# Gate and up products of pairs of inner tiles by Strassen's scheme (seven half-width products for eight), and the inner layer in groups of eight tiles

## Chip, core and metric

The kernel runs on one core of a Trainium2 chip. The metric is device time in microseconds (us) of one execution. Engine names are those of the profile: PE is the matrix engine (PEld its weight load), DVE the vector engine, ACT the scalar engine, POOL the general-purpose engine, SP the engine whose queue issues most transfers.

## What is computed

Six layers (four of a first block, two of a second) of a residual network over 512 positions and 1024 features, in float32. Each layer adds a mixer (attention, a state-space layer, a pooling layer or a hybrid) and then a gated feed-forward part to `x`. Only the feed-forward part is touched by the change; it has 2816 inner features:

```python
def swiglu(h, w_gate_up, w_down):
    g, u = jnp.split(h @ w_gate_up, 2, axis=-1)
    return (jax.nn.silu(g) * u) @ w_down
...
        x = x + swiglu(rms_norm(x, ffn_norm_g[i]), ffn_w_gate_up[i], ffn_w_down[i]).astype(x.dtype)
```

## The kernel before

**Layout.** Everything is kept feature-major: a tile has 128 features in the partitions and the 512 positions in the free dimension. `x` is eight such tiles (`KD` = 8); the inner layer of the feed-forward part has 22 (`KF` = 22).

**Three products for one.** A float32 operand is split into a high part rounded to the matrix engine's reduced format and a low part, the rest. `p3` multiplies high by high, high by low and low by high into one accumulator, so each 128x128 weight tile costs three matmuls of 512 columns. The split of the weights is made on the chip: a chunk `wraw` of eight weight tiles (128x1024 floats, 512 KB) comes by a transfer on SP's queue, ACT copies it to the high part `wh` (`w_h`), and DVE subtracts to get the low part `wl` (`w_l`). Chunks are used in strict order; `w_upto` keeps up to four of them in flight.

**The feed-forward part** (`ffn`). For each inner tile f a gate product `pg` and an up product `pu` are accumulated over the eight feature tiles (24 matmuls each). `close` then multiplies the gate by the row of reciprocal norms `rstd` (DVE), applies silu (ACT), multiplies by the up product (DVE), multiplies by `rstd` again (POOL, line 367) and `keep` splits the result into `ph` and `pl`, which hold all 22 inner tiles. When all are there, the down product runs: eight output tiles `po`, each over 22 inner tiles (66 matmuls), each added to `x`, after which the next layer's normalised tiles `Xh`, `Xl` are made. In the two layers of the second block the norm is applied beforehand, and `close` has no `rstd`.

**Side work.** Independent work of other layers is cut into steps in a queue `bg`, and `bgstep(nbg)` runs some of them in `close` and after each output tile. During the first layer these are the state-space layer's tables (names beginning with `s5`); during the next two they are products for the second block's modulation: DVE instructions `adaj` that each read a 256 KB transfer `adaw`, with two buffers for it.

**Order.** The instructions of each engine are executed in the order in which the program lists them; an engine that waits for one instruction starts none behind it. A scheduler of the framework moves instructions of one engine past each other where no data forbids it. The third layer's feed-forward part has a `lead`: the pooling mixer's steps run between the products of its first three inner tiles.

Of the kernel before, what the change touches and what calls it, by code (L numbers as in the profile page):

```python
# [20 lines left out]
P = 128  # L21
# [10 lines left out]
NH = 1  # L32
HALF = CH // NH
SLOTS = 8
NCHUNK = 541
# [35 lines left out]
def kernel(  # L71
# [55 lines left out]
    st = {"slot": 0, "dma": 1, "h": 0, "l": 0}  # L127
    raws, hs, ls = {0: wraw0}, {}, {}

    def w_dma(c):  # L130
        raws[c] = wp.tile([P, CH], F32, name="wraw", tag="wraw", bufs=4)
        sp.dma_start(raws[c], wst[c])

    def half(c):
        return raws[c // NH][:, c % NH * HALF:(c % NH + 1) * HALF]

    def w_h(c):
        hs[c] = wp.tile([P, HALF], F32R, name="wh", tag="wh", bufs=3 * NH)
        a.activation(hs[c], half(c), AF.Copy)  # L139

    def w_l(c):
        ls[c] = wp.tile([P, HALF], F32R, name="wl", tag="wl", bufs=2 * NH)
        v.tensor_tensor(out=ls[c], in0=half(c), in1=hs[c].bitcast(F32), op=ALU.subtract)  # L143

    def w_upto(c):
        last = wst.shape[0] - 1
        for key, ahead, end, make in (("dma", c // NH + 3, last, w_dma), ("h", c + 3 * NH - 1, NH * last + NH - 1, w_h),
                                      ("l", c + 2 * NH - 1, NH * last + NH - 1, w_l)):
            while st[key] <= min(ahead, end):
                make(st[key])  # L150
                st[key] += 1

    def wnext(n, *ks):
        s0 = st["slot"]
        hn = SLOTS // NH
        assert len(ks) == n and s0 // hn == (s0 + n - 1) // hn
        c, o = divmod(s0, hn)
        if o == 0 or c not in hs:
            w_upto(c)
        keys.extend(ks)  # L160
        st["slot"] += n
        sl = slice(o * P, (o + n) * P)
        return hs[c][:, sl], ls[c][:, sl]
# [11 lines left out]
    def mm(o, l, r, s0, s1):  # L175
        pe.matmul(o, lhsT=l, rhs=r, start=s0, stop=s1)  # L176

    def p3(o, l, r, first, last):
        mm(o, l[0], r[0], first, False)
        mm(o, l[0], r[1], False, False)  # L180
        mm(o, l[1], r[0], False, last)
# [164 lines left out]
    def ffn(name_gu, name_dn, lay, deferred, post, nbg=3, lead=None, ada=None):  # L346
        with tc.tile_pool(name="ffn", bufs=1, reuse_waits="tile") as fp:
            ph = fp.tile([P, KF, S], F32R, name="ph")
            F0 = 3
            plo = [fp.tile([P, F0, S], F32R, name="pl0")]  # L350
            R = {}

            def pl(f):
                if f >= F0 and len(plo) == 1:
                    plo.append(fp.tile([P, KF - F0, S], F32R, name="pl1", tag="pl1", bufs=1))
                return plo[0][:, f, :] if f < F0 else plo[1][:, f - F0, :]

            def tmp():
                return fp.tile([P, S], F32, name="t1", tag="t1", bufs=3)

            def close(f, pg, pu):
                t_ = tmp()
                if deferred:
                    v.tensor_tensor(out=t_, in0=pg, in1=R["r"], op=ALU.mult)  # L364
                    a.activation(t_, t_, AF.Silu)
                    v.tensor_tensor(out=t_, in0=pu, in1=t_, op=ALU.mult)  # L366
                    g_.tensor_tensor(out=t_, in0=t_, in1=R["r"], op=ALU.mult)  # L367
                else:
                    a.activation(t_, pg, AF.Silu)
                    v.tensor_tensor(out=t_, in0=pu, in1=t_, op=ALU.mult)  # L370
                keep(f, t_)

            def keep(f, t_):
                a.activation(ph[:, f, :], t_, AF.Copy)
                v.tensor_tensor(out=pl(f), in0=t_, in1=ph[:, f, :].bitcast(F32), op=ALU.subtract)
                bgstep(nbg)
# [4 lines left out]
            def gu(t, which, f, k):  # L381
                p3(t, wnext(1, gu_key(which, f, k)), xk(k), k == 0, k == KD - 1)

# [15 lines left out]
            if lead:  # L399

                f0 = F0
                steps = lead(fp.tile([P, (KF - F0) * S], F32, name="lroom", tag="pl1", bufs=1), tmp)
# [10 lines left out]
            for f in range(f0, KF):  # L413
                pg, pu = acc("pg"), acc("pu")
                for which, t in enumerate((pg, pu)):
                    for k in range(KD):
                        gu(t, which, f, k)
                    if deferred and "c" not in R and not lead:
                        R["c"] = rstd_cols(nrm["sq"])
                    elif deferred and "r" not in R:  # L420
                        R["r"] = keep_rstd(rstd_rows(R["c"]))
                close(f, pg, pu)
            for m in range(KD):
                po = acc("po")
                for f in range(KF):
                    w = wnext(1, ("t", name_dn, lay, f * P, m * P))
                    p3(po, w, (ph[:, f, :], pl(f)), f == 0, f == KF - 1)
                post(m, po)
                bgstep(nbg)
# [640 lines left out]
    def pool_lead(lay, fin):  # L1070
# [5 lines left out]
        def lead(room, tmp):  # L1076
            bufs_ = [room[:, i * W_:(i + 1) * W_] for i in range(17)]
            for t_ in bufs_:
                g_.memset(t_[:, :PAD], 0.0)
            rest = room[:, 17 * W_:]  # L1080
# [651 lines left out]
    for m in range(KD):  # L1732
        split_scaled(m, col("mix_g", m), False)
        if m == 1:
            w_h(0)
            w_l(0)
            st["h"] = st["l"] = 1
# [23 lines left out]
    if stage():  # L1761
        ffn("ffn_w_gate_up", "ffn_w_down", 1, True, then(add_x, fd("mix_g", 2)))
    if stage() and stage():
        ffn("ffn_w_gate_up", "ffn_w_down", 2, True, then(add_x, fd("mix_g", 3)), lead=pool_lead(0, fd("ffn_g", 2)))
# [8 lines left out]
    if stage():  # L1773
        ffn("ffn_w_gate_up", "ffn_w_down", 3, True, then(add_x, mixer[0].post if upto > 8 else None))
    for lay in range(2):
        if stage():
            hybrid(lay, then(gated(lay, 2), feed[lay].post), mixer[lay])
        if stage():
            ffn("w_gate_up_2", "w_down_2", lay, False, then(gated(lay, 5), mixer[1].post if lay == 0 else None), ada=feed[lay])
# [143 lines left out]
```

## Time and profile before

| | us |
|---|---|
| median of 3 runs | 3521.31 (3516.45 to 3531.56) |
| the profiled execution's own time | 3519.53 |
| its span, first to last instruction | 3517.8 |
| granted clock of PE, mean over the span | 0.992 of full speed |
| PE busy in the span | 3450.8 |
| DVE busy in the span | 1978.5 |

The busy time of an engine is the time in which at least one of its instructions was under way. A matmul's record lasts longer than the step from one matmul to the next, since they are pipelined: what one costs is read from starts, not from durations. The same holds, less strongly, for DVE.

### The profile page before, as it was taken

Reading aid. Unit: us, or ns where it says so; the run is one execution under the profiler, and the core shown is the slowest. Engines: PE = TensorE matmul, PEld = TensorE weight load, DVE = VectorE, ACT = ScalarE, POOL = GpSimd, SP = SyncE. Lnnn points to the kernel's source line nnn. Section 1 sums busy time; section 2 is a strip of 40 time slices with the busy share of each in tenths; the row PEclk is TensorE's granted clock in tenths of the full one; section 3 lists DMA queues with packets and bytes.
Section 4 is the critical chain, followed back from the end, with each engine's and each line's share of the span. In section 5 each row is a group of like instructions: output and inputs, shape, how many; then the busy total and the mean of one; then the engine's idle time right before and its main releaser. Section 6 shows DMA issues by size and latency. Waiting matters only on the chain.

```text
span 3517.8 us, 44670 instructions
## 1 busy us (share of the span) xinstructions
PE 3450.8 (98%) x16676; PEld 2848.3 (81%) x16676; DVE 1978.5 (56%) x3826; ACT 1333.0 (38%) x2127; POOL 503.6 (14%) x595
## 2 busy tenths in 40 slices
PE   8999999989999989999999999999999999999999
PEld 6887778888888868888788888877888887788887
DVE  8876786365555577554766433386643337664332
ACT  4553333323332233223554333356432225643221
POOL 1102443021111031100001221122100002210000
PEclk9999999999999999999999999999999999999999
DMA  4422344483455425544322222221132222113232
GB/s 153 112 70 91 117 134 140 142 271 115 137 172 170 149 98 179 168 156 146 127 73 69 96 96 96 90 93 37 49 102 96 96 90 94 37 49 102 96 104 82
DMA packets 189145, 395.26 MB, mean 112 GB/s; under 512 B 57552, under 2 KB 84320, under 8 KB 186880
## 3 DMA queue, kind: packets, MB, share of 16 engines
q1 hardware_dynamic: 186592, 375.61, 33.1%
q10 hardware_dynamic: 2304, 16.78, 1.4%
q8 instruction: 131, 2.15, 0.3%
q14 instruction: 86, 0.70, 0.1%
q0 software_dynamic: 32, 0.02, 0.0%
HBM read 372.33 MB, written 24.20 MB: 113 GB/s over the span
## 4 chain that ended last, share of the span: by engine, by line
PE 72%; DVE 4%; ACT 2%; issue 1%; DMA 1%; POOL 1%; SPq 0%; POOLq 0%; DVEq 0%; ACTq 0%
PE po L176 21%; PE pu L176 16%; PE pg L176 16%; PE pgl L176 2%; PE pq L176 2%; PE pv L176 2%; PE sc L176 2%; PE pld L176 1%; PE pz L176 1%; PE pgu L176 1%; PE tp L468 1%; PE px L176 1%; PE pV L176 1%; PE py L176 1%; DVE wl L143 1%
## 5 line engine op out<-in xcount | busy, mean ns | idle before, releaser
L143 DVE TENSOR_TENSOR wl<-wraw,wh 128x1024 fp32r<-128x1024 f32 x541 | 677.0, 1252 | 588.4 <-PE po L176 208.4
L139 ACT ACTIVATE wh<-wraw 128x1024 fp32r<-128x1024 f32 x541 | 572.4, 1059 | 1053.2 <-PE po L176 387.2
L176 PE MATMUL pu<-Xh,wh 128*128 128x512 f32 x1064 | 416.4, 391 | 0.0
L176 PE MATMUL pu<-Xl,wh 128*128 128x512 f32 x1064 | 415.9, 391 | 0.2 <-DVE Xl L312 0.2
L176 PE MATMUL pu<-Xh,wl 128*128 128x512 f32 x1064 | 415.6, 391 | 0.4 <-DVE wl L143 0.4
L176 PE MATMUL po<-ph,wl 128*128 128x512 f32 x1056 | 411.2, 389 | 1.0 <-DVE wl L143 1.0
L176 PE MATMUL po<-ph,wh 128*128 128x512 f32 x1056 | 411.3, 389 | 0.0
L176 PE MATMUL po<-pl,wh 128*128 128x512 f32 x1056 | 410.9, 389 | 0.0
L176 PE MATMUL pg<-Xh,wh 128*128 128x512 f32 x1000 | 391.8, 392 | 1.4 <-DVE t L364 1.4
L176 PE MATMUL pg<-Xl,wh 128*128 128x512 f32 x1000 | 390.6, 391 | 2.2 <-DVE Xl L312 2.2
L176 PE MATMUL pg<-Xh,wl 128*128 128x512 f32 x1000 | 389.7, 390 | 0.0
L303 POOL TENSOR_TENSOR sqa<-sqa,sqt 128x512 f32<-128x512 f32 x72 | 112.4, 1562 | 1236.4 <-ACT sqt L302 1235.6
L176 PEld LDWEIGHTS pu<-Xh,wl 128*128 128x128 f32 x1064 | 200.6, 189 | 42.8 <-DVE wl L143 1.2
L176 PEld LDWEIGHTS pu<-Xl,wh 128*128 128x128 f32 x1064 | 200.5, 188 | 41.8 <-DVE Xl L312 0.6
L176 PEld LDWEIGHTS pu<-Xh,wh 128*128 128x128 f32 x1064 | 200.4, 188 | 41.8 <-issue 0.6
L176 PEld LDWEIGHTS po<-ph,wl 128*128 128x128 f32 x1056 | 198.2, 188 | 42.8 <-DVE wl L143 1.4
L176 PEld LDWEIGHTS po<-ph,wh 128*128 128x128 f32 x1056 | 198.2, 188 | 41.3 <-issue 0.4
L176 PEld LDWEIGHTS po<-pl,wh 128*128 128x128 f32 x1056 | 198.2, 188 | 41.1 <-issue 0.2
L367 POOL TENSOR_TENSOR t<-t,rstd 128x512 f32<-128x512 f32 x88 | 134.2, 1526 | 665.8 <-DVE t L366 663.1
L176 PEld LDWEIGHTS pg<-Xh,wh 128*128 128x128 f32 x1000 | 187.9, 188 | 43.4 <-issue 3.2
L176 PEld LDWEIGHTS pg<-Xl,wh 128*128 128x128 f32 x1000 | 187.8, 188 | 42.2 <-DVE Xl L312 3.3
L176 PEld LDWEIGHTS pg<-Xh,wl 128*128 128x128 f32 x1000 | 187.8, 188 | 39.0 <-issue 0.2
(500 smaller groups left out, 5881.0 us busy)
## 6 DMA issues: line engine op xcount, KB each, us to landing
wraw<-in_wst_dram SPq DMA_DIRECT2D x541, 512.0 KB, 3.3
adaw<-in_wada_dram SPq DMA_DIRECT2D x192, 256.0 KB, 3.1
cbc<-c_d SPq DMA_DIRECT2D x32, 256.0 KB, 3.3
tbbr<-br_d ACTq DMA_DIRECT2D x8, 1024.0 KB, 6.2
tbct<-ct_d ACTq DMA_DIRECT2D x8, 1024.0 KB, 5.8
ct_d<-s5cp SPq DMA_DIRECT2D x128, 32.0 KB, 1.9
br_d<-s5ev SPq DMA_DIRECT2D x32, 128.0 KB, 2.0
ct_d<-kp_d SPq DMA_DIRECT2D x32, 128.0 KB, 2.8
```

What stands on the lines that cost most here:

```text
L139: a.activation(hs[c], half(c), AF.Copy)
L143: v.tensor_tensor(out=ls[c], in0=half(c), in1=hs[c].bitcast(F32), op=ALU.subtract)
L176: pe.matmul(o, lhsT=l, rhs=r, start=s0, stop=s1)
L303: (v if m == KD - 1 else g_).tensor_tensor(out=nrm[key], in0=nrm[key], in1=q, op=ALU.add)
L367: g_.tensor_tensor(out=t_, in0=t_, in1=R["r"], op=ALU.mult)
L468: pe.transpose(t_[:, j * P:(j + 1) * P], pr[:, j * P:(j + 1) * P], ident)
```

## The change

**Pairs by seven products.** Two inner tiles f, f+1 against two feature tiles k, k+1 and the two halves of the positions make a 2x2 by 2x2 block product. Before, it took eight products of half the width (as four of full width, 512). Strassen's scheme takes seven products of 256 columns, of sums of weight tiles with sums of halves of the normalised tiles. `pair(f)` does this for gate and up: seven units j = 0 to 6 of 24 matmuls each, into two accumulators `qa` and `qc` per product, with partial results copied out by ACT (`p1`, `p5`, `u2`) and added by DVE. Pairs named in `plain` are still computed the old way. 42 of the 66 pairs of the six layers go by seven products: 5, 8, 7, 8, 7 and 7.

**Weights.** For such a pair the four chunks hold the four blocks. Three of the seven units use a chunk as it comes; for the other four, DVE makes a sum `ws` of two (`w_s`). Each unit then has its own `wh` and low part `wsl`, so the pair has seven splits for four. A new planner `pump` replaces `w_upto`; it issues transfers, sums, high parts and low parts ahead of use, up to two units ahead for low parts. A chunk's buffer (there are four) is free for the next transfer once its last reader, a sum or a split, is done.

**Sums of the normalised tiles.** `sums(kp)`, once for each of four pairs of feature tiles in each layer, makes four sums of halves (two on DVE, two on POOL), and splits them into `T` (ACT and DVE).

**Groups of eight.** Inner tiles go in groups of 8, 8 and 6: gate and up of a group, then the down product of the group for all eight output tiles, each added to `x`. So each layer has three down phases for one, with 24, 24 and 18 matmuls for an output tile. The second multiplication by `rstd` moves from POOL (once for each inner tile) to DVE (once for each output tile and group, `t` from `po`). `bgstep` is called in `close` of plain tiles and after each output tile, not in `pair`; with `nbg` 6 in the first layer where it was 8.

```diff
-    def w_upto(c):
...
+    def w_s(i):
+        u = unit(i)
+        c, j = u["c"], u["j"]
+        if j is None or j in PLAIN:
+            return
+        t_ = ss[i] = room_of["quads"].tile([P, CH], F32, name="ws", tag="ws", bufs=NSS)
+        if j == 1:
+            tt(t_, raws[c + 1], raws[c + 2], ALU.add)
+        elif j == 2:
+            tt(t_, ss[i - 1], raws[c], ALU.subtract)
+        elif j == 3:
+            tt(t_, raws[c + 3], ss[i - 1], ALU.subtract)
+        else:
+            tt(t_, raws[c], raws[c + 1], ALU.subtract)
...
-                    v.tensor_tensor(out=t_, in0=pu, in1=t_, op=ALU.mult)
-                    g_.tensor_tensor(out=t_, in0=t_, in1=R["r"], op=ALU.mult)
...
+            def sums(kp):
...
+                tt(f_[:, 0], b_[0][:, hi_], b_[0][:, lo_], ALU.subtract)
+                tt(f_[:, 2], b_[1][:, hi_], b_[0][:, hi_], ALU.subtract, g_)
+                tt(f_[:, 1], b_[1][:, hi_], f_[:, 0], ALU.subtract)
+                tt(f_[:, 3], b_[1][:, lo_], f_[:, 1], ALU.subtract, g_)
+                a.activation(T["h"][:, kp], f_, AF.Copy)
+                tt(T["l"][:, kp], f_, T["h"][:, kp].bitcast(F32), ALU.subtract)
...
+                for j in range(7):
+                    l = quad_next(c, j)
+                    for which in range(2):
...
+                        o = (C if j % 2 else A)[which]
+                        for kp in range(4):
+                            at = (which * 4 + kp) * P
+                            p3(o, tuple(t[:, at:at + P] for t in l), right(j, kp), kp == 0 and j in (0, 1, 5), kp == 3,
+                               j in (2, 3, 4, 6))
...
-            for m in range(KD):
-                po = acc("po")
-                for f in range(KF):
...
+                for m in range(KD):
+                    po = acc("po")
+                    for f in g:
+                        w = wnext(1, ("t", name_dn, lay, f * P, m * P))
+                        p3(po, w, H[f], f == g[0], f == g[-1])
+                    if deferred:
+                        t_ = tmp()
+                        tt(t_, po, R["r"], ALU.mult)
+                        po = t_
+                    upd(m, po)
...
-            ffn("ffn_w_gate_up", "ffn_w_down", 0, True, then(add_x, fd("mix_g", 1, True)), nbg=8)
+            ffn("ffn_w_gate_up", "ffn_w_down", 0, True, add_x, fd("mix_g", 1, True), nbg=6,
+                plain=(0, 4, 8, 10, 14, 18))
```

The second layer (layer 1, `plain` 0, 10, 18) has pairs by seven products at f = 2, 4, 6, then 8, then 12, 14, then 16 and 20: a pair that comes right behind another is called a follower here. Layers 1 and 3 have three followers each (4, 6, 14), the third layer and the two of the second block (`plain` 0, 2, 10, 18) two each (6, 14), the first layer none: 12 in all.

On DVE, in layer 1 before, this stands from the close of one inner tile to the next (`wl` is a chunk's low part, `t` and `pl` belong to `close` and `keep`, `adaj` is side work):

```order
L366 TENSOR_TENSOR t_8808<-pu,t_8808 128x512
L375 TENSOR_TENSOR pl_8571<-t_8808,ph 128x512
L1182 SCALAR_TENSOR_TENSOR adaj,adap<-adaw,cbc 128x512
L143 TENSOR_TENSOR wl<-wraw,wh 128x1024
L1182 SCALAR_TENSOR_TENSOR adaj,adap<-adaw,cbc 128x512
L364 TENSOR_TENSOR t_8889<-pg,rstd 128x512
```

Now, at the same engine, between the middle of the pair f = 2 and the start of the pair f = 4 behind it (the first row is the low part of unit 6 of the first pair; `G`, `U` from `qa`, `qc` are partial results, `ws` from `wraw` alone is the next pair's first sum):

```order
L181 TENSOR_TENSOR wsl<-wraw,wh 128x1024
L284 TENSOR_TENSOR G_9522<-qa,p5g 128x256
L284 TENSOR_TENSOR G_9522<-G_9522,rstd 128x256
L284 TENSOR_TENSOR U<-qa,p5u 128x256
L284 TENSOR_TENSOR ws<-wraw 128x1024
L181 TENSOR_TENSOR wsl<-wraw,wh 128x1024
L284 TENSOR_TENSOR ws<-ws,wraw 128x1024
L284 TENSOR_TENSOR G_9521<-qc,p1g 128x256
L284 TENSOR_TENSOR U<-qc,p1u 128x256
L284 TENSOR_TENSOR G_9521<-G_9521,rstd 128x512
L284 TENSOR_TENSOR G_9522<-G_9522,U 128x256
L181 TENSOR_TENSOR wsl<-ws,wh 128x1024
```

What moved in: the sums, and a second pair's sums and splits stand between the first pair's partial results, in one queue.

At the start of layer 2's first such pair (f = 4), where the last of the four `T` is made, DVE has this order now (there was no such place before):

```order
L470 TENSOR_TENSOR t_13626<-pg,rstd 128x512
L284 TENSOR_TENSOR ws<-wraw,ws 128x1024
L1393 SCALAR_TENSOR_TENSOR adaj,adap<-adaw,cbc 128x512
L284 TENSOR_TENSOR T<-U,T 128x1024
L1393 SCALAR_TENSOR_TENSOR adaj,adap<-adaw,cbc 128x512
L284 TENSOR_TENSOR U<-G_13615 128x256
L474 TENSOR_TENSOR t_13626<-pu,t_13626 128x512
L1393 SCALAR_TENSOR_TENSOR adaj,adap<-adaw,cbc 128x512
L284 TENSOR_TENSOR U<-G_13616,U 128x256
L464 TENSOR_TENSOR pl_13631<-t_13626,ph_13630 128x512
L181 TENSOR_TENSOR wsl<-ws,wh 128x1024
L284 TENSOR_TENSOR T<-U,T 128x1024
```

Here the third and fourth `T` have moved in behind the close of the last plain tile (`t` from `pu`) and between pieces of side work.

## Rows read from the trace of the kernel before

**Rows 1.** The page, engines: busy us, share of span, instructions.

```profile
PE 3450.8 (98%) x16676; PEld 2848.3 (81%) x16676; DVE 1978.5 (56%) x3826; ACT 1333.0 (38%) x2127; POOL 503.6 (14%) x595
```

**Rows 2.** Chain of waits in layer 1: start us, us, what.

```profile
904.77 5.48 PE pg L176 x24
910.24 5.44 PE pu L176 x24
...
1133.28 119.68 PE po L176 x528
```

**Rows 3.** Windows, layer 1: length, then busy PE, PEld, DVE, ACT, POOL.

```profile
904.80:1133.30 228.50, 228.50 (x1009) 189.18 (x1008) 131.12 (x228) 71.42 (x87) 27.04 (x21) 1.00 0.51 166
1133.30:1253.00 119.70, 119.70 (x529) 99.11 (x529) 59.84 (x86) 32.20 (x37) 10.45 (x12) 1.00 0.46 149
```

**Rows 4.** Timeline of PE in a hybrid mixer: start us, duration us, 256-wide matmuls.

```profile
2333.02 0.28 PE L176 MATMUL pk<-wh,kvn 128*128 128x256 f32 x1
2333.14 0.28 PE L176 MATMUL pk<-wl,kvn 128*128 128x256 f32 x1
...
2333.38 0.34 PE L176 MATMUL pq<-wh,qn 128*128 128x384 f32 x1
...
2429.18 0.28 PE L176 MATMUL pk<-wh,kvn 128*128 128x256 f32 x1
...
2429.41 0.28 PE L176 MATMUL pk<-wh,kvn 128*128 128x256 f32 x1
```

**Rows 5.** Timeline around layer 2's lead: weight loads and matmuls of 128 columns, then f = 3.

```profile
1318.42 1.09 PEld L176 LDWEIGHTS nps<-cst,rc 128*128 128x128 f32 x8
1318.65 1.05 PE L176 MATMUL nps<-cst,rc 128*128 128x128 f32 x8
...
1320.37 1.89 DVE L364 TENSOR_TENSOR t<-pgu,rstd 128x512 f32<-128x512 f32 x3 [2.56 <-ACT rstd L333]
...
1321.12 0.50 PE L176 MATMUL pg<-Xh,wh 128*128 128x512 f32 x1 [1.41 <-DVE t L364]
```

**Rows 6.** Timelines of DVE: back-to-back instructions, 1024 wide and 512 wide.

```profile
315.05 1.23 DVE L143 TENSOR_TENSOR wl<-wraw,wh 128x1024 fp32r<-128x1024 f32 x1 [1.44 <-PE pg L176]
316.19 0.68 DVE L366 TENSOR_TENSOR t<-pu,t 128x512 f32<-128x512 f32 x1
...
804.26 0.68 DVE L197 TENSOR_TENSOR w<-pb,tbbr 128x512 f32<-128x512 f32 x1
804.86 0.68 DVE L197 TENSOR_TENSOR Xl<-ym,Xh 128x512 fp32r<-128x512 f32 x1
```

**Rows 7.** Groups of instructions on DVE by shape: busy us, mean ns, idle before.

```profile
L143 DVE TENSOR_TENSOR wl<-wraw,wh 128x1024 fp32r<-128x1024 f32 x541 | 677.0, 1252 | 588.4 <-PE po L176 208.4 <-PE pg L176 138.3 <-issue 106.1
...
L473 DVE COPY pt<-tp 128x512 f32<-128x512 f32 x24 | 16.4, 682 | 1.0 <-PE tp L468 1.0
...
L473 DVE COPY pt<-tp 128x256 f32<-128x256 f32 x24 | 10.0, 419 | 2.8 <-PE tp L468 2.5
```

**Rows 8.** DMA issues by line: count, KB each, median us from issue to landing.

```profile
wraw<-in_wst_dram SPq DMA_DIRECT2D x541, 512.0 KB, 3.3
...
tbbr<-br_d ACTq DMA_DIRECT2D x8, 1024.0 KB, 6.2
```

**Rows 9.** Timeline of layer 1's side work: SP's issue, and DVE's wait for it.

```profile
1126.60 0.33 SPq L1168 DMA_DIRECT2D adaw<-in_wada_dram  x1
...
1128.24 0.68 DVE L364 TENSOR_TENSOR t<-pg,rstd 128x512 f32<-128x512 f32 x1
1129.35 0.69 DVE L1182 SCALAR_TENSOR_TENSOR adaj<-adaw,cbc 128x512 bf16<-128x512 f32 x1 [0.43 <-DMA adaw<-in_wada_dram]
```

**Rows 10.** Groups of DVE in layer 0's down product: state-space tables, mean ns.

```profile
L197 DVE TENSOR_TENSOR s5bl<-s5bl,s5tw 128x128 f32<-128x128 f32 x8 | 3.6, 448 | 0.1
L197 DVE TENSOR_TENSOR s5bb<-s5bb,s5t 128x16 f32<-128x16 f32 x8 | 3.1, 392 | 0.0
```

**Rows 11.** Groups of POOL: the multiplication in `close`.

```profile
L367 POOL TENSOR_TENSOR t<-t,rstd 128x512 f32<-128x512 f32 x88 | 134.2, 1526 | 665.8 <-DVE t L366 663.1 <-DMA wraw<-in_wst_dram 2.7
```

More of the change, by code (lines that the diff above doesn't have):

```diff
@@ L145, in w_upto @@
-    def w_upto(c):
[L146 to L151, printed above, removed]
+    def w_s(i):
[10 more added lines that the diff above has]
+            tt(t_, raws[c + 3], ss[i - 1], ALU.subtract)
+        else:
+            tt(t_, raws[c], raws[c + 1], ALU.subtract)
@@ new lines, in raw_free, with sum_free @@
+    def raw_free(c):
+        for d in range(4):
+            if c - d in unit_of and (d == 0 or units[unit_of[c - d]]["j"] == 0):
+                i = unit_of[c - d]
+                if units[i]["j"] is None:
+                    return st["l"] > i
+                return st["s"] > i + 4 if d < 2 else st["l"] > i + (6 if d == 2 else 5)
+        return False
+    def sum_free(i):
+        u = units[i]
+        if u["j"] is None or u["j"] in PLAIN:
+            return True
+        return "quads" in room_of and st["l"] > i - (2 if u["j"] > 2 else 5)
@@ new lines, in pump @@
+    def pump(i):
+        u = unit(i)
+        most = u["c"] + (3 if u["j"] is None else 8)
+        moved = True
+        while moved:
+            moved = False
+            c = st["dma"]
+            if c <= min(most, LAST) and (c < NRAW or raw_free(c - NRAW)):
+                w_dma(c)
+                st["dma"] += 1
+                moved = True
+            k = st["s"]
+            n_ = unit(k)
+            if k <= i + 4 and n_["c"] + (0 if n_["j"] is None else QUAD_NEEDS[n_["j"]]) < st["dma"] and sum_free(k):
+                w_s(k)
+                st["s"] += 1
+                moved = True
+            k = st["h"]
+            if k < st["s"] and k <= i + NHI - 1:
+                w_h(k)
+                st["h"] += 1
+                moved = True
+            k = st["l"]
+            if k < st["h"]:
+                n_, key, most_l = unit(k), *(("nl", NLO) if unit(k)["j"] is None else ("nq", NSL))
+                if n_[key] < u[key] + most_l + (0 if (u["j"] is None) == (n_["j"] is None) else 1):
+                    w_l(k)
+                    st["l"] += 1
+                    moved = True
@@ L153, in wnext @@
     def wnext(n, *ks):
         s0 = st["slot"]
[L155 to L159, printed above, removed]
+        assert len(ks) == n and s0 // SLOTS == (s0 + n - 1) // SLOTS
+        c, o = divmod(s0, SLOTS)
+        while c not in unit_of:
+            unit(len(units))
+        i = unit_of[c]
+        assert units[i]["j"] is None
+        if o == 0 or i not in ls:
+            pump(i)
@@ L173, in walign, with mm, p3 @@
             st["slot"] += 1
[L175 to L181, printed above, removed]
+    def mm(o, l, r, s0, s1, onto=False):
+        pe.matmul(o, lhsT=l, rhs=r, start=s0, stop=s1, skip_group_check=onto)
+    def p3(o, l, r, first, last, onto=False):
+        mm(o, l[0], r[0], first, False, onto)
+        mm(o, l[0], r[1], False, False, onto)
+        mm(o, l[1], r[0], False, last, onto)
     LOG2E, LN2H, LN2L = 1.4426950408889634, 0.693145751953125, 1.428606765330187e-06
@@ L399, in ffn @@
             if lead:
-                f0 = F0
-                steps = lead(fp.tile([P, (KF - F0) * S], F32, name="lroom", tag="pl1", bufs=1), tmp)
+                f0 = 3
+                W_ = S + 16
+                lr = room(16 * S, "lroom")
+                steps = lead([lr[:, i * W_:(i + 1) * W_] for i in range(15)] + [gt(i, W_) for i in range(2)], lr[:, 15 * W_:], tmp)
                 pp = [(acc if i < 4 else scp)("pgu") for i in range(2 * f0)]
@@ L1778 @@
         if stage():
-            ffn("w_gate_up_2", "w_down_2", lay, False, then(gated(lay, 5), mixer[1].post if lay == 0 else None), ada=feed[lay])
+            ffn("w_gate_up_2", "w_down_2", lay, False, gated(lay, 5), mixer[1].post if lay == 0 else None, ada=feed[lay],
+                plain=(0, 2, 10, 18))
     for k in range(KD):
```

209 lines of the change are left out of this document (159 added, 50 removed).

## The prediction

> **What bounds the kernel now.** The engine table comes first: PE is busy for 98% of the span, DVE for 56% [rows 1]. The chain of waits then shows what PE does in a feed-forward part: every gate or up product of layer 1 is one piece of 24 matmuls that takes 5.44 us, piece after piece with nothing between, and the down product one piece of 528 in 119.68 us [rows 2]. Both give 0.2267 us for a matmul of 512 columns. The windows say the same: PE is busy for all of 228.5 and of 119.7 us there, while DVE has 131 of 228 us of work [rows 3]. So in these parts only fewer or shorter matmuls, or a wait of PE that is new, move the end. A pair of inner tiles costs 4 pieces, 21.76 us.
>
> **What is removed.** A pair by seven products has 7 x 24 = 168 matmuls of 256 columns. The kernel has such matmuls, with the same kind of split operands: three steps from start to start take 0.36 us (2333.02 to 2333.38) and two take 0.23 (2429.18 to 2429.41) [rows 4]: 0.115 to 0.12 each, and I take 0.1185. Then a pair costs 168 x 0.1185 = 19.91 us: 1.85 less, not the 2.72 that an eighth would be, since a matmul of half the width costs more than half of 0.2267. For 42 pairs that is **-78 us**. Bounds: the shortest step of PE in the trace with a weight load for each matmul is the run of eight of 128 columns, 1.05 to 1.09 us, 0.13 each [rows 5]; if a stream of 168 ran no faster than that, a pair would cost 21.8 and the gain be nothing. I take the row of the same width.
>
> The Trainium skill ("TensorE: Matmul & The Clock Gate", section on the back-to-back issue gap) puts the isolated step at columns/2.4 GHz plus 2.5 ns, 109 ns for 256 columns. By that a pair would cost 18.3 us, an estimate from that page, and the gain would be 145 us. For 512 columns the same rule gives 216 ns where the pieces above show 227, so the row decides.
>
> **What DVE gets for it.** Steps from start to start are 1.14 us for 1024 columns and 0.60 for 512 [rows 6]; for 256 the duration is 419 against 682 ns [rows 7], so I estimate 0.60 - 0.26 = 0.34. A pair with `rstd` has 4 sums and 7 low parts of 1024 (12.5 us), 4 instructions of 512 (2.4) and 10 of 256 (3.4): **18.3 us** in 19.9. It fits, barely, if DVE never waits. ACT's share is far smaller: seven copies of weights and eleven short ones, where it now has 71 us in 228 [rows 3].
>
> **A pair alone** (after plain tiles or a down phase) starts with its first three low parts and sums made in advance: some six of the eleven large instructions lie under PE's work before. It then needs under 12 us of DVE in 19.9. I cost its waits at nothing.
>
> **A follower** can't prepare. Its first sum needs its third chunk, whose buffer is free only when the pair before has made its unit 6's low part; that waits for unit 3 of that pair to leave the low-part buffer. The loop, by the order of DVE's queue: transfer 3.3 us to landing [rows 8]; first sum, low part 0, second sum 3 x 1.14; four partial results of unit 5, 3 x 0.34 + 0.60; low part 1, 1.14; `G` times `U` 0.60; third sum 1.14; `pl` 0.60; a 256 0.34; low part 2 1.14; a 256 0.34; fourth sum 1.14; `pl` 0.60; low part 3 1.22; unit 3 on PE, 24 x 0.1185 = 2.84; its partial result 0.42; low part 6 1.22. Sum 21.1 us, 1.2 over PE's 19.9. Twelve followers: **+14**. If the third chunk shares the queue with the fourth, its landing is nearer to the 6.2 us of 1024 KB [rows 8]: loop 24.0, +49. I take the lower, as transfers of one queue are issued one after the other; +49 is an end of the range.
>
> **Side work.** `adaj` reads a transfer that can be issued only after the instruction two before it: issued at 1126.60, used at 1129.35 [rows 9], 2.75 us, plus its own 0.69, is two in some 3.5 us. Before, three came in 10.88 us of gate and up. Now three come after each output tile, in 24 x 0.2267 = 5.44 us, and in the last group in 18 x 0.2267 = 4.08. The order leaves eight of layer 1 behind its last group, in the lead of layer 2, which DVE bounds: 8 x 0.60 = **+5**. The eight left by layer 2 stand between weight splits of the attention: +1.
>
> **Seams from a down phase to a pair.** In layers 3 to 5 the low part of unit 1 stands ahead of the last output tile's multiplication: no wait. In layers 1 and 2 side work has pushed it behind. After PE's last `po`, DVE has the multiplication, an `adaj`, the addition, a sum, an `adaj` (4 x 0.60 + 1.14) and the low part (1.22): 4.8 us, where unit 1 starts after 2.84: 1.9. At the second seam it stands ahead, and some 1 us is lost later. Four seams: **+7**. In layer 0, whose only such seam leads to f = 16, fifteen table instructions of 0.23 to 0.45 us [rows 10] stand there too: the low part comes at 9.2 us, 6.3 late, and about 3 more is lost at units 3 and 4: **+9**.
>
> **First pair of a layer.** `T` must be ready when unit 1 starts. In layers 0, 1 and 3 the fourth `T` stands behind the close of the second plain tile: 0.60 + 1.14 + 1.22, 3.0 us after PE leaves it, and its part of unit 1 comes after 2.84 + 1.07: in time. Layer 2 has only one plain tile (10.88 us) between its lead and f = 4. DVE is released at 1320.37 and PE starts f = 3 at 1321.12 [rows 5]. Until the fourth `T` the order has 12 instructions of close at 0.60, two of the last three `T`, sums and low parts at 1.14 (eight in all) and five of 256, besides nine `adaj` at 0.60: 7.2 + 9.1 + 1.7 + 5.4 = 23.4 us, to 1343.8. PE needs it at 1321.1 + 10.9 + 3.9 = 1335.9: **+8**.
>
> **The second multiplication** leaves POOL, where it took 1526 ns of each inner tile [rows 11], off the path. On DVE it adds one 0.60 to the end of four layers: **+2**. Without side work DVE has 0.60 + 0.60 + 1.14 for an output tile, in the last group also `Xl` but only three quarters of a split: under PE's 4.08. The down product keeps its matmuls. One chunk of weights more is nothing.
>
> **Sum:** 14 + 5 + 1 + 7 + 9 + 8 + 2 = 46 of new waits. 3519.5 - 78 + 46 = **3487.5 us** on the profiled execution's own time, which lies 1.8 under the median of the runs shown: I say 3488 (-0.9%). A change under 0.5%, some 17.6 us, can't be told from none here.
>
> **Rivals.**
> *Nearly all is hidden:* landings and seams fit, 0 to 15 us of waits: 3442 to 3457. For it: DVE's 18.3 is under 19.9. Against it: the loop of the followers. I take 0.17.
>
> *DVE paces the pairs* (the other side). Its steps are shorter than its durations only while instructions follow each other without a wait. By durations a pair is 11 x 1.22 + 4 x 0.69 + 10 x 0.42 = 20.4, and some fourteen of its instructions wait for ACT or PE; at 0.1 us each, an estimate, 21.8. If that held for each of the 42 pairs, the gain would be gone and 32 us of the other waits stay: 3552. It decides from 21.0 us a pair on (21.76 - 32/42). Against it: the pairs that can prepare, 30 of 42. I take 0.15.
>
> *PE's step stays at 0.13:* no gain, 46 of waits, 3566. The rows of that width speak against it: 0.04.
>
> *The step is 109 ns:* PE gains 143 us, DVE's 18.3 then equals PE's 18.3 and the waits are no smaller: 3519.5 - 143 + 46 = 3423. Rows 4 speak against it: 0.03. This is the skill's formula named above.
>
> **Numbers.** The forecast has 0.58, its own range 3460 to 3515; 0.12 of it lies within 0.5% of before. Of the pacing case 0.03 lies there too; 0.03 are left for what I don't see, half slower and half the same. Faster 0.17 + 0.46 + 0.03 = 0.66, same 0.165, slower 0.175. The range goes from 3442 (78 less, no wait) to 3544 (followers at 24.0, 35 more, and the 21 us of the side work's delay and the two kinds of seams doubled); outside are the 109 ns case and most of pacing and the 0.13 step, about 0.2.
>
> **What would show it.** A piece of 24 half-width matmuls in the chain takes 2.84 us where nothing waits; a pair alone 19.9, a follower about 21. PE's waits for `wsl` and `T` are new and add up to some 45 us; the longest piece stands at layer 2's f = 4, near 8 us. DVE is over 85% busy in a run of pairs. The prediction is wrong if a piece takes 3.1 us or more without a wait, if pairs alone wait too, or if PE waits in the down phases.

## The result, and the profile after

The changed kernel takes 3570.1 us (3565.9 to 3574.0); the kernel before took 3526.2 us beside it (3516.5 to 3531.6). The ratio is 1.0127, 95% interval 1.0098 to 1.0157: 1.3% slower, where 0.9% faster was forecast, and outside the range. The profiled execution took 3573.99 us, its span 3572.2 us.

The engines of the changed kernel (the columns of rows 1):

```profile
PE 3434.5 (96%) x19700; PEld 2963.9 (83%) x19700; DVE 2575.7 (72%) x4723; ACT 1591.6 (45%) x2607; POOL 457.7 (13%) x555
```

PE is busy for 16 us less than in [rows 1], but idle for 138 us where it was idle for 67. The pairs do what they should. The chain of waits in layer 3, where no side work runs (start us, us, what):

```profile
2074.09 43.55 PE po L263 x192
2137.79 5.47 PE pg L263 x24
...
2154.13 5.44 PE pu L263 x24
2199.89 43.55 PE po L263 x192
```

Between the first down phase (ending at 2117.64) and the next `pg` lies one pair: 20.15 us. Between the end of `pu` (2159.57) and the next down phase lie two, a pair and its follower: 40.32 us. That is 0.120 us a matmul, against 21.76 for a pair before [rows 2]: 1.61 us gained, 67.6 for 42. The down phase has its 192 matmuls at 0.2267 us, nothing between.

So 54.4 us more in the span, and 67.6 won, mean 122 us lost. (The medians differ by 43.9 only: the execution profiled before lies 6.7 us under its median, the one after 3.9 over. So some 10 us of the differences below are the spread of executions.) Of the 122, 71 are idle time of PE; the other 51 stand in its busy time, which should have fallen by 67.6 and fell by 16. By place, 52 of the 122 fall inside the 42 pairs, as far as these took over 20.15 us each. To see where, the span is cut at the first matmul of each stage (lengths in us, from PE's timeline; the runs in the last three columns come below):

| stage | before | after | groups alone | no adaj | late pairs, long last tiles |
|---|---|---|---|---|---|
| layer 0 | 401.2 | 426.8 | 417.2 | 424.0 | 409.3 |
| state-space layer | 197.3 | 204.8 | 203.3 | 205.5 | 194.0 |
| layer 1 | 361.0 | 362.3 | 363.1 | 352.0 | 361.7 |
| lead of layer 2 | 68.3 | 83.6 | 83.6 | 69.8 | 67.8 |
| rest of layer 2 | 326.6 | 334.1 | 326.6 | 319.9 | 330.2 |
| attention | 272.8 | 280.4 | 272.2 | 272.1 | 272.1 |
| layer 3 | 361.3 | 354.3 | 363.6 | 353.7 | 351.6 |
| first hybrid mixer | 268.0 | 280.3 | 280.2 | 280.1 | 272.1 |
| fifth part | 348.5 | 341.4 | 348.5 | 341.5 | 338.2 |
| second hybrid mixer | 266.9 | 266.7 | 266.7 | 266.6 | 266.7 |
| sixth part | 352.7 | 345.5 | 352.6 | 345.5 | 342.2 |

Only layer 3 and the last two parts gain, 7 us each. Four places lose: layer 0 with the state-space layer behind it, the lead, the rest of layer 2 with the attention behind it, and the first hybrid mixer, whose code did not change.

**Layer 0.** Windows of the changed kernel (the columns of rows 3; PEclk, the granted clock, is the third number from the end), layer 0 and the first hybrid mixer:

```profile
292.00:718.80 426.80, 401.64 (x2153) 334.05 (x2153) 333.93 (x691) 161.49 (x257) 145.34 (x194) 0.96 0.38 113
...
2338.30:2618.60 280.30, 266.10 (x1484) 222.72 (x1482) 185.97 (x363) 153.73 (x302) 62.03 (x75) 0.97 0.17 56
```

The same two windows of the kernel before:

```profile
293.40:694.50 401.10, 397.51 (x1793) 318.25 (x1792) 269.13 (x566) 130.79 (x198) 135.58 (x209) 0.99 0.40 124
...
2281.80:2549.80 268.00, 259.47 (x1484) 218.29 (x1482) 181.71 (x358) 149.88 (x297) 55.70 (x72) 0.99 0.18 59
```

In layer 0 PE is idle for 25.2 us instead of 3.6. In the hybrid mixer it is idle for 5.7 us more (14.2 against 8.5), and the same 1484 matmuls keep it busy for 6.6 us more, at a clock of 0.97 instead of 0.99. In layer 0, likewise, the idle time grew by 21.6 us, and the busy time by 4.1 where five pairs should have taken 8.1 off. So a wait is paid twice: once as idle time and once as slower matmuls behind it. What PE waits for in layer 0 (engine, line, producer: us in total, times, longest):

```profile
PE s5p L1040 <- DVE s5bl L284: 9.9, 9, 4.1
PE s5p L1040 <- ACT s5ev L1044: 7.8, 4, 3.1
```

`s5p` are PE's own products for the state-space tables: the side work stands in PE's queue too, and PE waits there for DVE's and ACT's part of it.

**Seams and lead.** DVE and PE at layer 1's seam to f = 16 (start us, duration, what, [idle before and releaser]):

```profile
1187.59 0.69 DVE L284 TENSOR_TENSOR t<-po,rstd 128x512 f32<-128x512 f32 x1
...
1191.40 0.69 DVE L1393 SCALAR_TENSOR_TENSOR adaj<-adaw,cbc 128x512 bf16<-128x512 f32 x1 [0.78 <-DMA adaw<-in_wada_dram]
...
1192.02 1.22 DVE L181 TENSOR_TENSOR wsl<-ws,wh 128x1024 fp32r<-128x1024 f32 x1
...
1193.30 0.58 PE L263 MATMUL qa<-T,wsl 128*128 128x256 f32 x1 [3.37 <-DVE wsl L181]
```

PE's down phase ended at 1183.77; DVE takes the last `po` 3.8 us later, and the low part waits behind. Until then its queue holds an addition, two `adaj`, a low part and a sum, one right behind the other; earlier in the down phase `adaj` had waited for transfers, longest for 2.23 and 1.26 us. The pair took 26.5 us. The other three seams of layers 1 and 2 were 1.8, 3.0 and 4.1 us over 20.15.

The groups of DVE, before and after (columns of rows 7):

```profile
L1182 DVE SCALAR_TENSOR_TENSOR adaj<-adaw,cbc 128x512 bf16<-128x512 f32 x192 | 143.7, 748 | 48.8 <-DMA adaw<-in_wada_dram 48.3
...
L1393 DVE SCALAR_TENSOR_TENSOR adaj<-adaw,cbc 128x512 bf16<-128x512 f32 x192 | 138.5, 721 | 42.1 <-DMA adaw<-in_wada_dram 40.5
```

DVE stands still for 40.5 us in front of `adaj`, with sums, low parts and `po` behind them in its queue. That is not new, it was 48.3 us before; what is new is that PE waits for what stands behind.

**The first hybrid mixer** begins with the norm of layer 3's output. DVE and PE at the end of layer 3:

```profile
2324.01 0.68 DVE L284 TENSOR_TENSOR t<-po,rstd 128x512 f32<-128x512 f32 x1
...
2328.92 0.75 DVE L399 SCALAR_TENSOR_TENSOR Xl<-x,facol,Xh 128x512 fp32r<-128x512 f32 x1 [1.39 <-ACT Xh L398]
...
2347.75 1.86 PE L263 MATMUL pc<-ones,sqa 128*128 128x1 f32 x8 [3.58 <-DVE sqa L390]
```

For each output tile DVE multiplies, adds, and then waits for ACT's squares and `Xh` before `Xl`. In the last group an output tile has 18 matmuls, 4.08 us, and DVE's round is longer (six rounds from 2314.59 to 2343.10, 4.75 us each): the norm is 3.6 us late, and the clock falls behind it. The second hybrid mixer lost nothing (266.7 us, 266.9 before), though the fifth part ends in tiles of 18 matmuls too; there DVE multiplies and adds in one instruction.

### The profile page after: what moved, and what is told of

The parts are those of the page before. It is cut to its first block, busy times and chain, and to the rows that moved or that the text cites. A ratio compares the mean times of both kernels' runs of the same rounds, so it can differ in the third digit from the quotient of the medians.

```text
span 3572.2 us, 52162 instructions
## 1 busy us (share of the span) xinstructions
PE 3434.5 (96%) x19700; PEld 2963.9 (83%) x19700; DVE 2575.7 (72%) x4723; ACT 1591.6 (45%) x2607; POOL 457.7 (13%) x555
## 4 chain that ended last, share of the span: by engine, by line
PE 72%; DVE 15%; DMA 5%; issue 3%; ACT 3%; POOL 1%; SPq 0%; POOLq 0%; DVEq 0%; ACTq 0%
PE po L263 18%; PE qa L263 12%; PE qc L263 9%; PE pu L263 6%; PE pg L263 5%; PE pq L263 4%; DMA adaw<-in_wada_dram 4%; PE pv L263 3%; PE pgl L263 2%; DVE wl L181 2%; PE sc L263 2%; DVE adaj L1393 2%; PE tp L681 1%; PE pld L263 1%; PE pz L263 1%
## 5 line engine op out<-in xcount | busy, mean ns | idle before, releaser
L181 DVE TENSOR_TENSOR wl<-wraw,wh 128x1024 fp32r<-128x1024 f32 x374 | 475.5, 1271 | 177.0 <-PE pgl L263 33.4
L263 PE MATMUL qa<-T,wh 128*128 128x256 f32 x2016 | 373.4, 285 | 0.6 <-ACT wh L174 0.6
L263 PEld LDWEIGHTS qa<-T,wh 128*128 128x128 f32 x2016 | 318.3, 194 | 1.0 <-ACT wh L174 1.0
L263 PE MATMUL qa<-T,wsl 128*128 128x256 f32 x1008 | 288.3, 286 | 11.9 <-DVE wsl L181 11.9
L181 DVE TENSOR_TENSOR wsl<-ws,wh 128x1024 fp32r<-128x1024 f32 x168 | 206.8, 1238 | 42.1 <-ACT wh L174 41.5
L263 PEld LDWEIGHTS qa<-T,wsl 128*128 128x128 f32 x1008 | 195.9, 194 | 13.5 <-DVE wsl L181 13.5
L263 PE MATMUL qc<-Xh,wsl 128*128 128x256 f32 x672 | 191.4, 286 | 1.9 <-DVE wsl L181 1.8
L263 PE MATMUL qc<-Xh,wh 128*128 128x256 f32 x672 | 190.9, 285 | 0.7 <-ACT wh L174 0.7
L1393 DVE SCALAR_TENSOR_TENSOR adaj<-adaw,cbc 128x512 bf16<-128x512 f32 x192 | 138.5, 721 | 42.1 <-DMA adaw<-in_wada_dram 40.5
L263 PE MATMUL pu<-Xh,wh 128*128 128x512 f32 x392 | 155.7, 397 | 1.8 <-ACT Xh L398 1.8
L263 PE MATMUL pu<-Xh,wl 128*128 128x512 f32 x392 | 155.4, 396 | 1.5 <-DVE wl L181 1.5
```

What stands on the lines that cost most here:

```text
L181: v.tensor_tensor(out=ls[i], in0=whole(i), in1=hs[i].bitcast(F32), op=ALU.subtract)
L263: pe.matmul(o, lhsT=l, rhs=r, start=s0, stop=s1, skip_group_check=onto)
L1393: tc.keep_in_program_order(v.scalar_tensor_tensor(out=j, in0=T.pop(i), scalar=1.0, in1=T["c"][:, (i % 2) * W:(i % 2) * W + W], op0=ALU.mul ...
```

## Experiments

Theory 1 is crowding: the work that hangs on an output tile or on side work has less of PE's time to hide under, so its chains come onto PE's path. Theory 2 is load: the pairs' sums and splits are too much for DVE.

**Groups alone.** `plain` holds every pair, and no sums are made.

```diff
-plain=(0, 4, 8, 10, 14, 18)
+plain=tuple(range(0, KF, 2))
```

> The groups of eight alone: every pair is computed the old way, and no sums of the normalised tiles are made. Theory 1 (crowding): what follows an output tile (state-space tables, adaj, the addition to x, squares and norms) now has 4 to 5.4 us of PE's work per output tile instead of 15, so its chains come out on PE's path, whatever way the pairs are computed. Then layer 0 still takes some 420 us against 401 before, the first hybrid mixer still loses some 12 us, and the kernel takes 3526 + 55 = 3580 us or more. Theory 2 (DVE is overloaded by the pairs' sums and splits): without them layer 0 falls to 401 to 405, the lead of layer 2 to 70, and the kernel takes 3526 to 3540 us.

It took 3575.6 us, ratio 1.0145 (1.0128 to 1.0161): grouping, with what the change has beside the pairs (the planner, the moved multiplication, six steps for eight), costs 53 us of span with no pair in it. By the table, 22 are in layer 0 and the state-space layer, 15 in the lead and 12 in the first hybrid mixer. Theory 1 holds for these. But what the pairs add on top is large too: they win 67.6 us and give back about as much, in layer 0 (18 us, after its own gain of 8), layer 1 (12), the rest of layer 2 (19) and the attention (8).

**Layer 0 whole.** Layer 0 as one group of 22, computed the old way, `nbg` 8; all else as changed.

```diff
-nbg=6, plain=(0, 4, 8, 10, 14, 18))
+nbg=8, plain=tuple(range(0, KF, 2)), sizes=(22,))
```

> The changed kernel, but layer 0 as before: one group of 22 inner tiles, all computed the old way, eight steps of tables in each close and output tile. Both theories: layer 0 falls from 427 to 401 us. Theory 1 says that the state-space layer behind it is also back at 197 us from 205 (it lost to the table work that layer 0 left late and to the short last output tiles), so 3570 - 33 = 3537 us. Theory 2 says that only layer 0 itself gains: 3570 - 25 = 3545 us.

3553.4 us, ratio 1.0075 (1.006 to 1.009): less than either expectation. Layer 0 took 408.6 us and the state-space layer 199.7, so 23 of the 33 us that the two had lost came back. The other 10 stay without groups and pairs in layer 0. The new planner, the scheduler's order, the moved multiplication and the low place of the one execution profiled before are left as causes; no run separates them.

**Tables first.** All table steps ahead of layer 0.

```diff
             bg.extend(s5_tables(bp, T5))
+            while bg:
+                bgstep()
```

> The changed kernel with all table steps of layer 0 listed ahead of its feed-forward part, so that they run in one burst about its first two inner tiles. If the tables alone make layer 0 long (PE's own products for them wait for DVE, ACT and transfers, 18 us by the trace, and the clock falls behind those waits), everything in layer 0 behind the burst runs clean: a down phase of 24 matmuls for an output tile takes 43.55 us, a pair 20.15, and the pair at f = 16, which took 33 us with its waits, also; the burst itself costs more than it saves, since nothing covers it, so the whole is slower, 3580 us or more. If groups and pairs are at fault, the down phases of layer 0 still take 51 us and more, and f = 16 over 25.

3665.4 us: the burst, with little over it, costs 95 us more. Behind it layer 0 is clean. Its chain of waits:

```profile
541.57 43.55 PE po L263 x192
...
623.20 5.44 PE pu L263 x24
...
648.79 5.47 PE pg L263 x24
...
670.57 43.52 PE po L263 x192
...
734.25 5.47 PE pg L263 x24
```

628.64 to 648.79 and 714.09 to 734.25 are single pairs, 20.15 and 20.16 us; with the tables between them the first down phase alone had taken 51 us. Behind the burst nothing of layer 0's loss is left: it comes with the tables. The state-space layer, though, took 205.4 us here too, with no table step left for it, so its 7.5 us are not theirs. Its new waits in the changed kernel are for `Xh`, `Xl` and `wl` at its head, 4.0 us where 0.2 were before:

```profile
PE pu L263 <- ACT Xh L398: 1.8, 1, 1.8
```

They are of the kind that heads the first hybrid mixer: a norm behind short last output tiles with the moved multiplication.

**Even tables.** Ten steps in each close and three after each output tile, instead of six and six.

```diff
-                    bgstep(nbg)
+                    bgstep(nbg if nbt is None else nbt)
```

> The changed kernel with layer 0's table steps laid more evenly over PE's time: ten in each close of a plain tile and three after each output tile, instead of six and six (192 calls in all, 216 before). Crowding (six steps in 5.44 us of an output tile are more than DVE, ACT and the queue can do, and PE waits for its own table products): layer 0 falls from 427 to 410 us or less, the whole to 3555 us. If it is the pairs' load on DVE, layer 0 stays within 4 us of 427.

3579.7 us, slower by 10. Layer 0 fell by 8 us only, to 418.4, and the state-space layer rose by 17 to 222.0; in the two, PE waited for `s5ev` 15.0 us instead of 7.8, and no longer for `s5bl` (9.9 in the changed kernel). So the rate after an output tile is not the whole cause: other waits in the tables' own chain took the place of those that went, and tables that end late are paid behind the layer. Layer 0 met neither expectation: crowding by the rate after an output tile alone is not borne out, and neither is the load of the pairs.

**No adaj.**

```diff
-            tc.keep_in_program_order(v.scalar_tensor_tensor(out=j, in0=T.pop(i), ...
+            if i == 0:
+                v.memset(part, 0.01)
```

> The changed kernel without the side work of layers 1 and 2: the 192 adaj instructions and their transfers are left out, and a constant stands for their sums. If adaj is what makes PE wait at the seams of layers 1 and 2 (14.8 us over the pairs' own time), at layer 2's f = 4 (9.5 us), in the lead (15 us more than before) and in the attention behind layer 2 (7.6 us more), most of these 47 us go: 3570 - 40 = 3530 us. If it is the pairs' own DVE work and the transfers of weights, under 12 us go: above 3558 us.

3527.7 us, ratio 1.0009 (0.9999 to 1.0018): 42 less. Windows of the lead and of the rest of layer 2:

```profile
1275.00:1344.80 69.80, 53.45 (x225) 40.76 (x223) 60.78 (x80) 33.64 (x47) 26.77 (x63) 0.93 0.18 61
1344.80:1664.70 319.90, 318.03 (x1944) 286.55 (x1945) 226.76 (x289) 137.08 (x195) 11.65 (x10) 0.99 0.30 99
```

In the rest of layer 2 PE is idle for 1.9 of 319.9 us. By the table, which compares the two profiled executions, layer 1 gains 10.3, the lead 13.8, the rest of layer 2 14.2 and the attention 8.3, together 46.6. The seams of layers 1 and 2 are 20.15 us each, as theory 1 has it: the pairs alone leave no wait there.

**adaj without its transfers.**

```diff
-                out=j, in0=T.pop(i), scalar=1.0, ...
+                out=j, in0=T["c"][:, 0:W], scalar=1.0, ...
```

> The changed kernel with all adaj instructions, which read a tile that is already there instead of 192 transfers of 256 KB; the transfers are left out. The run without adaj gained 42 us. Theory A (latency of the transfer: with two buffers, two adaj in 3.5 us, and DVE's queue waits for it): nearly all of that comes back here too, 3530 to 3536 us. Theory B (DVE's time for adaj itself, 0.6 us each, between sums and low parts): little comes back, 3560 us or more.

3546.0 us, ratio 1.0054 (1.0037 to 1.0071): 24 of the 42 us. Neither theory alone: what goes with the transfers is a little over half, DVE's time for `adaj` the rest. In layer 1 (353.8 us) it is nearly all the transfers; in the lead (77.7) time is the larger part. The four seams take 20.15 us each here, with all `adaj` in them, so the transfers make the seams' loss; layer 2's f = 4 still takes 25.9. Whether it is their latency or their share of the queue that brings the weights, this run can't tell: it takes both away.

**Late pairs.** Pairs only in the last three parts; layers 0 and 1 in one group, layer 2 in groups of 6 and 16, all the old way.

> Pairs by seven products only in the last three feed-forward parts, where there is no side work; layers 0 and 1 as before in one group of 22 inner tiles, layer 2 by groups of 6 and 16 the old way. The traces of the changed kernel give a gain of 7 us in each of the three parts, and a loss of 12 us in the first hybrid mixer. Theory 1: that loss comes with the short last output tiles and stays: 3526 - 21 + 12 + 2 = 3519 us. Theory 2: it comes with DVE's load and mostly stays too; but if it was only late side work of layers before, it goes, and the time is 3507 us.

3529.3 us, ratio 1.0006 (0.9995 to 1.0017): no gain. The 21 us came, the hybrid mixer took 280.7 us as theory 1 says, and two losses came that were not expected: 9 us in layer 2, whose first down phase now stood right behind the lead with `adaj` in it (a likely cause, not tested), and 12.5 in layer 0 and the state-space layer (407.6 and 203.4).

**Late pairs, long last tiles.** From that version: nine pairs in each of the last three parts, groups of 6, 8 and 8, so that the last output tiles have 24 matmuls; layer 2 in groups of 8, 8 and 6; in layers 0 and 1 the second multiplication back on POOL.

```diff
-plain=(0, 10, 18)
+plain=(0, 2), sizes=(6, 8, 8)
...
+                if len(sizes) == 1:
+                    g_.tensor_tensor(out=t_, in0=t_, in1=R["r"], op=ALU.mult)
```

> Layers 0 and 1 as the kernel before has them (one group, second multiplication on POOL), layer 2 in groups of eight the old way; pairs by seven products only in the last three feed-forward parts, nine in each instead of seven or eight, in groups of 6, 8 and 8: all four pairs of a group of eight follow each other. If a follower waits for nothing (the two pairs at f = 12 and 14 took 40.31 us), four take 80.6 us, each of the three parts gains 9 x 1.61 less some 4 us at its first pair, and the last output tiles with 5.44 us instead of 4.08 hold the norms' chain, so that the first hybrid mixer is back at 270 us from 280: 3527 - 31 + 2 = 3498 us. By the loop of the followers in the prediction (21.1 us each), 18 followers cost 18 us: 3516 us. If the hybrid mixer stays at 280, 10 us more in either case.

3497.8 us, ratio 0.9916 (0.9901 to 0.9931): faster than both kernels, and the expected number, but in part by luck: by the table the last three parts gain 30.5 us as expected, and layer 0 (8.1), the first hybrid mixer (4.1) and the rest of layer 2 (3.6) stay over the one execution profiled before, itself under its median. Windows over the first hybrid mixer and over four pairs in a row in layer 3 (columns as above):

```profile
2280.40:2552.50 272.10, 261.90 (x1484) 219.10 (x1482) 183.63 (x360) 151.40 (x298) 59.01 (x73) 0.99 0.18 57
...
2032.00:2112.70 80.70, 80.70 (x674) 80.66 (x674) 70.88 (x95) 44.84 (x69) 0.00 (x0) 1.00 0.34 112
```

The hybrid mixer's 1484 matmuls take 261.9 us of PE's time instead of 266.1, at a clock of 0.99: with a longer cover for the norm's chain neither the wait nor its echo in the clock is left, but for 4 us. Of the pairs, 672 matmuls in 80.64 us (2032.20 to 2112.84 in the chain), no wait, with DVE 88% busy: here a follower costs nothing.

**Two buffers for the tables' copies.** The last version with two `s5ev` and `s5evk`.

```diff
-                ev = mk("ev", shape=(P, 2 * NB2 * P))
+                ev = mk("ev", shape=(P, 2 * NB2 * P), bufs=2)
```

> The version with late pairs and long last output tiles, and two buffers instead of one for the two tiles by which ACT takes the tables' products off PSUM (s5ev, s5evk). In layer 0 of that version PE waited three times 1.8 us for s5ev, and the clock fell behind two of these waits. If the one buffer, which an outgoing transfer holds, is the cause, layer 0 falls from 409 to 402 us and the time from 3498 to 3491 us. If it is the order of ACT's queue (s5ev stands behind an activation of the close that waits for DVE), nothing moves: 3496 to 3500 us.

3506.4 us, ratio 0.9951 (0.9935 to 0.9968): slower by 9 than the version it comes from, which neither expectation has, with layer 0 at 413.0 us instead of 409.3. PE waits for `s5ev` still (1.8 and 1.2 us), and once for `s5bl` (3.4). So the one buffer is not what makes layer 0 long; that ACT's order is, is not shown by this.

**What a wait costs.** A chain on POOL holds the first pair behind a down phase, with six lengths.

```diff
+                            if hold:
+                                mm(A[which][:, 0:1], hold.pop(0)[:, 0:P], ones[:, 0:1], True, True)
```

> What a wait of PE costs: in the last three feed-forward parts a chain of POOL instructions of six lengths holds back the pair behind the first and the second down phase (which takes 20.15 us without a wait). If a wait costs its own length, the pair takes 20.15 us and the wait. If the clock falls behind longer waits, as the seam at layer 1's f = 16 suggests (3.4 us of wait, 6.3 us longer), waits up to about 2 us cost themselves alone, and each longer one 2 to 4 us more, whatever its length.

3602.5 us in one run. PE's timeline, the held matmuls, with the idle time before them:

```profile
2116.29 0.38 PE L263 MATMUL qa<-ones,dly 128*128 128x1 f32 x2 [2.89 <-POOL dly L650]
...
2885.02 0.59 PE L263 MATMUL qa<-ones,dly 128*128 128x1 f32 x2 [5.10 <-POOL dly L650]
...
3374.55 0.58 PE L263 MATMUL qa<-ones,dly 128*128 128x1 f32 x2 [3.29 <-POOL dly L650]
3503.06 0.38 PE L263 MATMUL qa<-ones,dly 128*128 128x1 f32 x2 [0.48 <-POOL dly L648]
```

These pairs took 25.01, 27.81, 26.75 and 21.11 us. Less 20.15 and the wait, that leaves 2.0, 2.6, 3.3 and 0.5 us. The shortest chain (a wait of 0.13) left 0.5 as well, 20.77 us in all. In the pair of the longest, PE waited 1.08 us for a high part, 1.95 for a low part and 4.57 for the chain: 31.20 us, 3.4 left. The windows behind the waits of 0.48 and of 3.29:

```profile
3503.00:3509.00 6.00, 5.94 (x49) 5.94 (x50) 3.73 (x4) 3.00 (x5) 0.01 (x1) 1.00 0.44 152
...
3374.50:3382.00 7.50, 7.45 (x38) 7.46 (x39) 0.58 (x1) 2.05 (x5) 0.00 (x0) 0.57 0.39 140
```

The granted clock of the second is 0.57, nearly all at the lower level (1.2 GHz), and 38 matmuls take what 62 take at 0.120 us. The two short waits left 0.5 us each at the full clock, so about that much belongs to the held matmuls themselves; behind the waits of 2.89, 3.29 and 5.10 us some 1.5, 2.8 and 2.1 us are the clock's (estimates by difference).

The length of a wait does not settle it alone. In layer 0 of the version with late pairs and long last tiles PE waits three times for `s5ev`, 1.78, 1.78 and 1.72 us, up to 413.48, 491.38 and 567.56. Windows behind them:

```profile
414.00:420.00 6.00, 5.37 (x17) 3.82 (x16) 4.85 (x13) 2.04 (x4) 2.36 (x6) 0.72 0.29 75
492.00:498.00 6.00, 5.37 (x25) 3.93 (x23) 5.38 (x14) 1.94 (x4) 2.81 (x6) 1.00 0.38 89
569.50:575.50 6.00, 5.10 (x12) 4.08 (x13) 5.44 (x15) 0.62 (x3) 3.04 (x6) 0.52 0.33 66
```

Behind the first and the third the clock fell, behind the second it did not.

## Why the prediction was wrong

- **What bounds the kernel:** right. PE sets the end, and only new waits and shorter work move it.
- **The pairs' gain, -78:** mechanism right, size off: -67.6, as the step is 0.120 and not 0.1185. A pair has 20.15 us, the forecast 19.91. Of the two rows that were averaged, the one of three steps had 0.120. The 0.13 of the 128-wide row was a misreading: it divides a record with its tail by eight, and from start to start that run steps at 0.111. The 109 ns by the formula of the Trainium skill (TensorE: Matmul & The Clock Gate, back-to-back issue gap), which the page gives for an isolated matmul, did not hold for this stream.
- **A pair alone costs no wait:** right behind down phases in layers 3 to 5, wrong at the first pair of layer 1 (2.9 us), of layer 3 (1.1) and of the last two parts (3.8 and 3.7): the last `T` and the low parts meet on DVE there. The prediction let the `T` of layers 1 and 3 be in time, and did not look at the last two parts.
- **A follower, +14:** wrong, 2.8 for all twelve, of which 1.3 and 0.3 at layer 3's f = 4 and 6, right behind the first pair, and nothing at the others of the last three parts. The loop's first step failed. Around f = 14 of layer 3 (SP's issues, unit 6's low part, the follower's first sum):

```profile
2170.52 0.33 SPq L151 DMA_DIRECT2D wraw<-in_wst_dram  x1
2172.10 1.22 DVE L181 TENSOR_TENSOR wsl<-wraw,wh 128x1024 fp32r<-128x1024 f32 x1 [0.48 <-ACT wh L174]
2173.35 0.33 SPq L151 DMA_DIRECT2D wraw<-in_wst_dram  x1
2174.03 1.22 DVE L284 TENSOR_TENSOR ws<-wraw 128x1024 f32<-128x1024 f32 x1
```

  The first sum starts 0.7 us after the low part ends, too early for a transfer of 3.3 us in between. The transfer that did wait for this low part (2173.35) is the fourth chunk's; the third chunk's had been issued at 2170.52, into another chunk's buffer.
- **Seams, +7, and layer 2's f = 4, +8:** places right, sizes 15 (1.8, 6.3, 3.0 and 4.1 over 20.15) and 9.6. (The seams' own terms, 1.9 and 1 in each of two layers, add up to 6 and not 7.) That the transfers of `adaj` set the seams was not in the sum.
- **Down phases don't wait:** right in layers 1 to 5: 192 matmuls took 43.5 to 44.5 us. Wrong in layer 0.
- **Layer 0, +9:** the step that failed most. Only one seam was costed, as if the tables were DVE's work alone. That seam's pair, f = 16, took 32.8 us, 12.6 over 20.15. But the tables have products on PE too, which wait for DVE and ACT (9.9 and 7.8 us), all over the layer: 33.7 us were lost over the pairs' gain. The 7.5 in the layer behind, which stay when the tables are done first, had no term.
- **Side work in the lead +5, in the attention +1:** 15.3 and 7.6. Eight instructions were counted in the lead at 0.60 us of DVE; the trace has fourteen there, where three were before, and the run without transfers shows that 5.9 of the 15.3 go with the transfers.
- **Second multiplication, +2:** costed as one instruction at four ends. What counts is the whole round of an output tile, 4.75 us, against 4.08: 12.3 us in the first hybrid mixer, of which 8 to 9 come back with 5.44 us (280.7 to 272.1).
- **No term for the clock:** the sum added waits at their own length. The mean granted clock fell from 0.992 to 0.979: some 46 us of full clock more than before that PE did not have, part of it while it was idle. Of the 122 us lost, 51 are in PE's busy time.
- **Rivals:** DVE pacing the pairs, which was to give 3552, is refuted: four pairs in a row run at 20.16 us, with DVE busy for 17.7 us a pair (the prediction's sum: 18.3). That the change is slower came from a case that was not among them: many short waits and the clock behind them, 52 us inside the pairs, nearly all at first pairs and at seams, and 70 outside.

The ledger: -67.6 for the pairs; +34 tables (layer 0); +47 `adaj`; +12 the first hybrid mixer and +7 the state-space layer, at the norms; the remaining 22 lie in what is left of layers 1 to 3 and of the last two parts, 4 to 6 us in each, about half of it at its first pair. Sum 54. The first two losses are shown by runs that take the work away or move it, the 12 by the run that gives the last tiles their length back; the cause at the state-space layer is argued from its waits. Of the 34, 22 are idle time of PE and 12 slower busy time; what the planner and the scheduler's order have in them stays open.

## What to carry to other kernels

When PE is 98% busy, a saving in PE's main products is worth what the covered work leaves of it: before costing a change, list all that hides under the stage, on every engine's queue and PE's own, and compare each round with the shorter time that it will have. Cutting one long phase into short ones shortens all covers at once. Put the faster scheme first where nothing is hidden (here the last three parts, 0.9916), and keep the last tiles before a norm long.

## What was not expected of the hardware

Waits of PE of 2.89, 3.29 and 5.10 us cost some 1.5, 2.8 and 2.1 us beyond themselves through the clock, between 1.4 and 1.9 times their length in all; behind waits of 0.13 and 0.48 us the clock stayed, and of three waits of 1.7 to 1.8 us it fell behind two. The Trainium skill (TensorE: Matmul & The Clock Gate, HAM oscillation) tells of waits for transfers behind which PE is throttled again. Here the clock fell behind waits for POOL (0.57 behind that of 3.29 us) and for ACT too.

In the pairs the weight loads are under way all the time: PEld 80.66 of 80.70 us, where the wide products had 189 of 228 [rows 3]. The Trainium skill (Perfetto Trace Analysis, Identifying the Most-Contended Engine) takes the share of peak arithmetic and the weight loads' busy share, not the matmuls', for the measure of distance to the limit. Here the full share proves no limit: a load's record lasts 0.19 us, so records overlap at a step of 0.120. And matmuls of one column, each with a weight load of 128 columns, follow each other faster, in the kernel before (eight records; the eight starts lie between 2285.38 and 2286.16, a step of 0.112):

```profile
2285.38 1.03 PE L176 MATMUL pc<-ones,sqa 128*128 128x1 f32 x8
```

So the loads alone do not set the 0.120. From 512 to 256 columns the step falls by 0.107, from 0.2267 to 0.120; carried on in a straight line, an estimate, 0.013 us of each matmul do not shrink with its width. That is why half the width costs more than half: what this part is, no run shows.
